# Hybrid decoder layer on one core: the recurrence's half of the output projection moved between the steps of the prompt attention

## The chip, the cores and the metric

One Trainium2 chip, one core. The metric is the device time of one execution in microseconds. A profile of one execution gives the rows below; times in the trace count from its first instruction.

## The reference

One step of a decoder layer for a prompt of 2048 tokens and a sample group of 8 sequences of 8 tokens, in float32, model width 1024:

```
n = rms_norm(x);  proj = n @ w_in
att = dilated_attention(q, k, v)      # 8 heads x 64; windows (128,1), (512,4), (2048,16)
rw  = rwkv7_time_mix(...)             # 8 heads x 64, recurrence over the tokens
h = x + concat(att, rw) @ w_out       # w_out: 1024 x 1024
y = h + relu(rms_norm(h) @ w_mlp1)**2 @ w_mlp2
```

The mixture has 1024 features: 512 from the attention (`att`), 512 from the recurrence (`rw`). The product with `w_out` is a sum over both, so either half can be made alone and added later. Each sample sequence also attends over 2048 cached keys and values.

## The kernel before, in words

Features lie on the 128 partitions, tokens run along the free axis: 2048 prompt tokens and 64 sample tokens, 2112 columns. Products that must keep float32 accuracy are made of two fp32r parts, "high" and "low": hi = round(x), lo = x - hi (`split`: a copy on ScalarE, line 185, a subtraction on VectorE, line 182), and three matmuls hi x hi, hi x lo, lo x hi.

The order of the work is: input projection and recurrence, to about 1200 us; the prompt attention; the output projection with the sample's attention inside it; the feed-forward part. Intermediate results go through DRAM: `mixA` (four panels of 128 features from the attention) and `mixR` (four from the recurrence, complete before the attention begins).

**Prompt attention** (`attention`, line 1053). Four passes p, one for each pair of heads (`ty` 0 and 1), each with three branches b and four groups of token blocks. A step is two blocks of 128 queries in branches 0 and 1, four in branch 2; so a pass has 8 + 8 + 4 = 20 steps, and all passes 80. In a step the scores of a block are made by two matmuls (lines 1084 and 1085, tile `sc`), bias and row minimum on VectorE (line 1087), the exponential on ScalarE (line 185, tile `e`), transposes on TensorE (line 1102, tile `pt`), a copy to SBUF by ScalarE and VectorE in turn (`evac`, tile `pts`), and the product with the values (line 1109, tile `o`). After each step `pump()` draws two pieces of `merge` of the pass before, a generator of about 20 pieces: it weights the three branches by their softmax denominators (matmul line 1197 into the one PSUM buffer of pool `pax`, tile `ax`; products on VectorE, sums on GpSimd, line 1200) and stores to `mixA`. The last pass's merge runs after the loop, on the score banks, and its sums on VectorE. Value tiles `vt` (line 1039) are loaded three ahead into four buffers; the next pass's keys and queries during branches 1 and 2.

**Output projection** (from line 1426 on). Six chunks of 352 columns (`NC_`). `wo_panel` loads and splits a panel of 128 rows of the weight (two of the eight in pool `we` during the last pass, six in the buffers that the last pass's keys leave); `mix_panel` loads and splits a panel of the mixture for one chunk. Each chunk loads the input `xh` into its part of the residual (line 1441), and for each of 8 groups of 128 output features makes 8 panels x 3 = 24 matmuls (line 1451, tile `pwo`, four PSUM buffers), in the order of panels 4 to 7 (recurrence), 0 to 3 (attention); VectorE adds the result to the residual (tile `res`). After each group two pieces of the **sample's attention** are drawn (`sample_all`, line 1312, 8 sequences of 8 pieces). A sequence reads 5 key tiles and 5 value tiles of 512 KB from the cache (`kv`, lines 1255 and 1288; two buffers in pool `sat` and two in `wo2`, in turn) and 8 rows of new values. The last chunk holds the 64 sample columns, so all of the sample comes before it. From the third chunk on the residual is stored to `hD` (line 1457).

All transfers are issued by SP, in one order. The framework's scheduler fixes each engine's order when the program is built, by priority (program order) and a simulated timeline; an engine then works in that order.

Of the kernel before, what the change touches and what calls it, by code (L numbers as in the profile page):

```python
# [171 lines left out]
def _build(ctx, tc, nc, I, O, dbg, upto):  # L172
# [49 lines left out]
    mixR = dram.tile([4, P, T + NS], F32, name="mixR")  # L222
    hD = dram.tile([P, KT, T + NS], F32, name="hD")
# [758 lines left out]
    ar = ph2.enter_context(pool(name="ar", bufs=1))  # L982

# [40 lines left out]
    def bias_load(p, b):  # L1024
        bts = []
        for ty in range(2):
            bt = ae.tile([P, 256], F32, name=f"bt{b}{ty}")
            nc.sync.dma_start(out=bt, in_=bass.AP(tensor=bvD.tensor, offset=bvD.offset + (2 * p + ty) * P * 1152 + b * 384 + 127, ap=[[1151, P], [1, 256]]))
            bts.append(bt)
        return bts  # L1030
# [22 lines left out]
    def attention(p, pump, ahead):  # L1053
# [5 lines left out]
        for b in range(3):  # L1059
# [8 lines left out]
            for grp in range(4):  # L1068
                vp, vt = vt, next_v()
                o = ppo.tile([P, 512], F32, name="o")  # L1070
                for t2 in range(0, 4, 2 if b < 2 else 4):
# [3 lines left out]
                    for ty in range(2):  # L1075
# [4 lines left out]
                        for x, i in enumerate(tl):  # L1080
# [6 lines left out]
                            V.tensor_tensor_reduce(out=e[:, c0:c0 + n], in0=ps[:, c0:c0 + n], in1=bts[ty][:, 256 - n:256], scale=-1.0, scalar=3e38, op0=ALU.add, op1=ALU.min, accum_out=nm)  # L1087
# [36 lines left out]
    def merge(p, ob, st):  # L1124
# [47 lines left out]
        dn = at.tile([P, P], F32, name="dn")  # L1172
        dm = at.tile([P, P], F32, name="dm")
# [52 lines left out]


    kvs = []

    def kv_tile():  # L1230

        kv_tile.n += 1
        pl, bufs = kvs[kv_tile.n % len(kvs)]
        return pl.tile([P, 1024], F32, name="kv", bufs=bufs)
# [86 lines left out]
    woh = [None] * KT  # L1321
    wol = [None] * KT
# [9 lines left out]
    def mix_panel(pl, k, c0):  # L1332

        mh = pl.tile([P, NC_], F32R, name="mh", bufs=5)
        ml = pl.tile([P, NC_], F32R, name="ml", bufs=5)
        src = (mixA if k < 4 else mixR)[k % 4]
        n = min(NC_, (T if k < 4 else NT) - c0)
        mr = we.tile([P, 512], F32, name="mr", tag="raw", bufs=3)
        nc.sync.dma_start(out=mr[:, :n], in_=src[:, c0:c0 + n])
        split(mr[:, :n], mh[:, :n], ml[:, :n])  # L1340
        if n < NC_:
            split(attS[:, k], mh[:, n:], ml[:, n:])
        return mh, ml

    rest = iter(())
    for p in range(4):
        before = rest
        def pump():
            for _ in range(2):
                next(before, None)  # L1350

        rest = attention(p, pump, ahead)
        for _ in before:
            pass
        if p == 2:
            kqa.close()
            we = ph3.enter_context(pool(name="we", bufs=1, side="right"))
            sat = ph3.enter_context(pool(name="sat", bufs=1, side="right"))

# [23 lines left out]
    kvs.append((sat, 2))  # L1383
    for k in (4, 5):
        wo_panel(we.tile([P, 2 * D], F32R, name=f"wo{k}"), k)
    mixed = {}
    for k in range(4, 8):
        mixed[k, 0] = mix_panel(we, k, 0)
# [37 lines left out]
    with pool(name="wo2", bufs=1) as wo2, pool(name="pwo", bufs=4, space=PSUM, side="right") as pwo, pool(name="psa", bufs=1, space=PSUM) as psa, pool(name="pst", bufs=1, space=PSUM) as pst:  # L1426
        kvs.append((wo2, 2))
        sample = sample_all(psa)
        for k in (6, 7, 0, 1, 2, 3):
            wo_panel(kqb.tile([P, T], F32R, name="wo", tag="kq"), k)  # L1430
        order = (4, 5, 6, 7, 0, 1, 2, 3)
        for c0 in range(0, NT, NC_):
# [8 lines left out]
            nc.sync.dma_start(out=h, in_=I["xh"][:, :, c0:c0 + NC_])  # L1441
            for k in order:
                if (k, c0) not in mixed:
                    mixed[k, c0] = mix_panel(we if k >= 4 else wo2, k, c0)
            for o in range(KT):
                ps = pwo.tile([P, 512], F32, name="pwo")
                i = 0
                for k in order:
                    mh, ml = mixed[k, c0]
                    for a, b in ((woh, mh), (woh, ml), (wol, mh)):  # L1450
                        PE.matmul(ps[:, :NC_], a[k][:, o * P:(o + 1) * P], b, start=(i == 0), stop=(i == 3 * KT - 1))  # L1451
                        i += 1
                tt(h[:, o], ps[:, :NC_], h[:, o], ALU.add)
                for _ in range(2):
# [219 lines left out]
```

## Time and profile before

| what | us |
|---|---|
| median of 3 runs | 3351.66 |
| lowest and highest | 3347.38 and 3363.11 |
| the profiled execution | 3357.47 |
| its span, first to last instruction | 3355.7 |

The span leaves out 1.8 us of the profiled execution's own time. A row of a view of groups has line, engine, operation, output and inputs, shapes, the count, then busy time and mean of one, then idle time of the engine before them and what ended it. PE is TensorE's matmuls, PEld its weight loads, which overlap them; DVE, ACT and POOL are VectorE, ScalarE and GpSimd; SPq is SP's queue.

### The profile page before, as it was taken

To read this page: it belongs to the slowest core of one execution; us is meant where nothing else is said; L and a number is where in the kernel's file an instruction comes from. 1 tells how busy PE (TensorE), PEld (TensorE's weight loads), DVE (VectorE), ACT (ScalarE), POOL (GpSimd) and SP (SyncE) were. 2 spreads that over 40 slices of the span, in tenths; PEclk is the share of its full clock that TensorE was granted. 3 is DMA by queue.
4 is the path that set the end of the run, shared out by engine and by line. 5 is a ranking of instruction groups with operands and counts; after the bars stand their busy time and mean duration, and the time that the engine had idled before them with its cause. 6 is when DMAs were issued, how large, how long until landed. Compare 5 with 4: busy or idle time off the path is not lost.

```text
span 3355.7 us, 63761 instructions
## 1 busy us (share of the span) xinstructions
PE 3135.5 (93%) x24214; PEld 2865.0 (85%) x24214; DVE 2157.2 (64%) x4547; ACT 1469.2 (44%) x3497; POOL 976.1 (29%) x1141
## 2 busy tenths in 40 slices
PE   5999899989988979999799689999999999999999
PEld 5876877877787868888688579999899999899999
DVE  4656677677566435656554577676976767967675
ACT  4545566555555446677222233232433323433332
POOL 1003422453044100111000233343533334533332
PEclk9999999999998989999899789999999999999999
DMA  5465575466456383323766322222232222222222
GB/s 169 137 185 149 131 204 158 109 157 178 124 131 178 106 279 117 126 74 90 243 221 235 123 85 89 64 85 64 98 113 64 88 63 86 88 68 84 64 89 73
DMA packets 349144, 418.55 MB, mean 125 GB/s; under 512 B 117252, under 2 KB 210367, under 8 KB 348837
## 3 DMA queue, kind: packets, MB, share of 16 engines
q1 hardware_dynamic: 348836, 414.48, 41.6%
q8 instruction: 190, 3.11, 0.4%
q14 instruction: 118, 0.96, 0.1%
HBM read 325.62 MB, written 93.46 MB: 125 GB/s over the span
## 4 chain that ended last, share of the span: by engine, by line
PE 72%; DMA 9%; DVE 9%; SPq 3%; issue 2%; POOL 2%; ACT 2%; DVEq 0%; POOLq 0%; ACTq 0%
PE pm L1603 20%; PE pm L1557 17%; PE pj L334 7%; PE pwo L1451 5%; PE pj L802 4%; PE o L1109 3%; PE pt L1102 2%; PE sc L1084 2%; PE sc L1085 2%; DVE ml L182 2%; DMA wr<-in_wq 1%; DMA wr<-in_wr 1%; DVE rl L1517 1%; DVE wl L1477 1%; DMA xg<-in_xg 1%
## 5 line engine op out<-in xcount | busy, mean ns | idle before, releaser
L185 ACT ACTIVATE wh<-wr 128x512 fp32r<-128x512 f32 x744 | 463.4, 625 | 818.5 <-PE pm L1603 473.4
L1603 PE MATMUL pm<-fh,wl 128*128 128x352 f32 x1536 | 495.9, 323 | 8.8 <-DVE wl L1477 8.8
L1603 PE MATMUL pm<-fh,wh 128*128 128x352 f32 x1536 | 493.4, 324 | 0.0
L1603 PE MATMUL pm<-fl,wh 128*128 128x352 f32 x1536 | 492.6, 323 | 0.5 <-DVE fl L182 0.5
L1557 PE MATMUL pm<-ml,wh 128*128 128x352 f32 x1344 | 437.0, 325 | 15.1 <-DVE ml L182 15.1
L1557 PE MATMUL pm<-mh,wh 128*128 128x352 f32 x1344 | 438.6, 327 | 9.4 <-ACT mh L185 9.2
L1557 PE MATMUL pm<-mh,wl 128*128 128x352 f32 x1344 | 436.0, 325 | 5.7 <-DVE wl L1477 4.6
L182 DVE TENSOR_TENSOR res<-pm,res 128x352 f32<-128x352 f32 x384 | 198.6, 522 | 287.5 <-PE pm L1603 284.7
L1477 DVE TENSOR_TENSOR wl<-wr,wh 128x512 fp32r<-128x512 f32 x432 | 361.1, 836 | 6.1 <-ACT wh L185 3.5
L1603 PEld LDWEIGHTS pm<-fh,wl 128*128 128x128 f32 x1536 | 290.2, 189 | 9.8 <-DVE wl L1477 9.8
L1603 PEld LDWEIGHTS pm<-fl,wh 128*128 128x128 f32 x1536 | 289.4, 189 | 1.3 <-DVE fl L182 1.1
L1603 PEld LDWEIGHTS pm<-fh,wh 128*128 128x128 f32 x1536 | 289.2, 189 | 0.8 <-ACT fh L185 0.2
L1557 PEld LDWEIGHTS pm<-ml,wh 128*128 128x128 f32 x1344 | 256.5, 191 | 19.1 <-DVE ml L182 19.0
L1557 PEld LDWEIGHTS pm<-mh,wh 128*128 128x128 f32 x1344 | 256.2, 191 | 11.5 <-ACT mh L185 11.5
L1557 PEld LDWEIGHTS pm<-mh,wl 128*128 128x128 f32 x1344 | 255.8, 190 | 8.9 <-DVE wl L1477 7.3
L802 PE MATMUL pj<-wh,nh 128*128 128x256 f32 (+1 forms) x816 | 242.4, 298 | 13.5 <-ACT qn L185 6.7
L802 PE MATMUL pj<-wh,nl 128*128 128x256 f32 (+1 forms) x816 | 241.1, 296 | 2.2 <-DVE nl L182 2.2
L334 PE MATMUL pj<-nh,wh 128*128 128x512 f32 (+3 forms) x600 | 222.8, 374 | 20.4 <-ACT nh L185 10.4
L1481 POOL TENSOR_TENSOR wr<-wr 128x512 f32<-128x512 f32 x48 | 68.9, 1435 | 591.0 <-DVE wl L1477 502.6
L802 PE MATMUL pj<-wl,nh 128*128 128x256 f32 (+1 forms) x816 | 240.7, 296 | 0.0
L182 DVE TENSOR_TENSOR wl<-wr,wh 128x512 fp32r<-128x512 f32 (+1 forms) x216 | 150.2, 698 | 135.2 <-ACT wh L185 130.0
L334 PE MATMUL pj<-nl,wh 128*128 128x512 f32 (+3 forms) x600 | 222.0, 371 | 5.9 <-DVE nl L182 5.9
(312 smaller groups left out, 7262.2 us busy)
## 6 DMA issues: line engine op xcount, KB each, us to landing
wr<-in_w SPq DMA_DIRECT2D x384, 256.0 KB
wr<-in_wr SPq DMA_DIRECT2D x120, 256.0 KB
wr<-in_wq SPq DMA_DIRECT2D x96, 256.0 KB
kv<-in_kc SPq DMA_DIRECT2D x40, 512.0 KB
kv<-in_vc SPq DMA_DIRECT2D x40, 512.0 KB
xsD<-xst SPq DMA_DIRECT2D x56, 256.0 KB
xrkv<-xsD SPq DMA_DIRECT2D x32, 384.0 KB
vt<-vD SPq DMA_DIRECT2D x48, 256.0 KB
```

The lines of the kernel that those rows point to most:

```text
L182: V.tensor_tensor(out, a, b, op)
L185: S.activation(out, in_, func, bias=bias, scale=scale, **kw)
L334: PE.matmul(ps[:m, :n], a[:, k, :m], b[h * 4 + k][:, c0:c0 + n], start=(h == 0 and i == 0), stop=(h == 1 and i == 11))
L802: PE.matmul(out, a[h * 2 + k][:, i * P:i * P + m], b[:, k, :], start=(h == 0 and q == 0 and i % 2 == 0), stop=(h == 3 and q == 5 and (i % ...
L1084: PE.matmul(ps[:, c0:c0 + n], cols(qst, b, i, False), cols(kst, b, i, both), start=True, stop=False)
L1085: PE.matmul(ps[:, c0:c0 + n], cols(qst, b, i, False), cols(klo, b, i, both), start=False, stop=True)
L1109: PE.matmul(o[ty * 64:ty * 64 + 64, (i % 4) * P:(i % 4 + 1) * P], kv[:, ty * 64:ty * 64 + 64], ptss[ty][:, y * P:(y + 1) * P], start=fst, ...
L1451: PE.matmul(ps[:, :NC_], a[k][:, o * P:(o + 1) * P], b, start=(i == 0), stop=(i == 3 * KT - 1))
L1477: (G if pooled else V).tensor_tensor(wl, w, wh.bitcast(F32), ALU.subtract)
L1481: G.tensor_tensor(S[0], A21, A22, ALU.add)
L1557: PE.matmul(ps, a[:, k], b[:, k], start=(n == 0), stop=(n == 11))
L1603: PE.matmul(ps, a[:, f], b[:, cs], start=(i == 0), stop=(i == 11))
```

## The change

A generator `recurrent_half` is added. Twice (for output features 0 to 511 and 512 to 1023) it loads and splits the weight rows of the four recurrence panels, then goes over 8 chunks of 264 columns: it loads and splits the four recurrence panels of the mixture (copy and subtraction both on GpSimd), and for each of 4 groups of output features loads the input, makes 4 x 3 = 12 matmuls into the attention's buffer `ax`, adds the input on VectorE and stores the sum to a new DRAM tensor `rD`. It yields twice for the weights of each half, once after each chunk's loads and once after each product: 2 x (2 + 8 x 5) = 84 times. `pump()` draws it once a step and twice in each eighth; what is left is drawn after the four passes.

The output projection then loads `rD` in place of the input and makes 12 matmuls for each group, over the attention's panels only. Its four weight panels all go into buffers that the last pass's keys leave, after the last merge in program order; two more of these buffers become four more tiles for the sample's cache, so that `kv` has eight. The sample's pieces are drawn 8 for each 5 groups, over five chunks. To make room, the third branch's bias tile is 128 columns wide and two small tiles share buffers of others.

```diff
@@ -220,6 +220,7 @@
     xsD = dram.tile([15, P, T + NS], F32, name="xsD")
     mixA = dram.tile([4, P, T + NS], F32, name="mixA")
     mixR = dram.tile([4, P, T + NS], F32, name="mixR")
+    rD = dram.tile([P, KT, T + NS], F32, name="rD")
     hD = dram.tile([P, KT, T + NS], F32, name="hD")
@@ -980,6 +981,7 @@
     at = ph2.enter_context(pool(name="at", bufs=1))
     ae = ph2.enter_context(pool(name="ae", bufs=1))
     ar = ph2.enter_context(pool(name="ar", bufs=1))
+    fo = ph2.enter_context(pool(name="fo", bufs=1))
     kqb = ph3.enter_context(pool(name="kqb", bufs=6, side="right"))
     kqs = [kqa.enter_context(pool(name="kqa", bufs=6)), kqb]
@@ -1024,8 +1026,9 @@
     def bias_load(p, b):
         bts = []
         for ty in range(2):
-            bt = ae.tile([P, 256], F32, name=f"bt{b}{ty}")
-            nc.sync.dma_start(out=bt, in_=bass.AP(tensor=bvD.tensor, offset=bvD.offset + (2 * p + ty) * P * 1152 + b * 384 + 127, ap=[[1151, P], [1, 256]]))
+            w = 256 if b < 2 else 128
+            bt = ae.tile([P, w], F32, name=f"bt{b}{ty}")
+            nc.sync.dma_start(out=bt, in_=bass.AP(tensor=bvD.tensor, offset=bvD.offset + (2 * p + ty) * P * 1152 + b * 384 + 383 - w, ap=[[1151, P], [1, w]]))
             bts.append(bt)
         return bts
@@ -1169,8 +1172,8 @@
             tt(alike(sc[:, b], b), alike(nall, b), nat(0, b), ALU.subtract)
         act(sc, sc, AF.Exp)
         yield
-        dn = at.tile([P, P], F32, name="dn")
-        dm = at.tile([P, P], F32, name="dm")
+        dn = at.tile([P, P], F32, name="dn", tag="nall2")
+        dm = at.tile([P, P], F32, name="dm", tag="nall")
         tt(dn, sc[:, 0], nat(1, 0), ALU.mult)
         for b in (1, 2):
             tt(alike(dm, b), alike(sc[:, b], b), nat(1, b), ALU.mult)
@@ -1224,14 +1227,52 @@
     G.memset(zst, 0.0)
     mv2 = at.tile([P, 2, 2, 4, 4, 8], F32, name="mv2")
+    FT = 264
+
+    def recurrent_half():
+
+
+        def halves(src, hi, lo):
+            n = src.shape[-1]
+            r = fo.tile([P, FT], F32, name="fr", bufs=3)
+            nc.sync.dma_start(out=r[:, :n], in_=src)
+            G.tensor_copy(hi, r[:, :n])
+            G.tensor_tensor(lo, r[:, :n], hi.bitcast(F32), ALU.subtract)
+
+        for o0 in range(0, KT, 4):
+            w = []
+            for k in range(4):
+                w.append([fo.tile([P, 512], F32R, name=f"fw{x}{k}") for x in "hl"])
+                for c in range(0, 512, 256):
+                    halves(I["wo"][:, 4 + k, o0 * P + c:o0 * P + c + 256], w[k][0][:, c:c + 256], w[k][1][:, c:c + 256])
+                if k % 2:
+                    yield
+            for c0 in range(0, T + NS, FT):
+                m = []
+                for k in range(4):
+                    m.append([fo.tile([P, FT], F32R, name=f"fm{x}", bufs=4) for x in "hl"])
+                    halves(mixR[k, :, c0:c0 + FT], *m[k])
+                yield
+                for o in range(4):
+                    x = fo.tile([P, FT], F32, name="fr", bufs=3)
+                    nc.sync.dma_start(out=x, in_=I["xh"][:, o0 + o, c0:c0 + FT])
+                    ps = pax.tile([P, 512], F32, name="ax")
+                    i = 0
+                    for k in range(4):
+                        for a, b in ((0, 0), (0, 1), (1, 0)):
+                            PE.matmul(ps[:, :FT], w[k][a][:, o * P:(o + 1) * P], m[k][b], start=(i == 0), stop=(i == 11))
+                            i += 1
+                    tt(x, ps[:, :FT], x, ALU.add)
+                    nc.sync.dma_start(out=rD[:, o0 + o, c0:c0 + FT], in_=x)
+                    yield
+
     kvs = []
     def kv_tile():
         kv_tile.n += 1
-        pl, bufs = kvs[kv_tile.n % len(kvs)]
-        return pl.tile([P, 1024], F32, name="kv", bufs=bufs)
+        return kvs[kv_tile.n % len(kvs)]()
     kv_tile.n = -1
@@ -1329,25 +1370,30 @@
             nc.sync.dma_start(out=wr, in_=I["wo"][:, k, o:o + 512])
             split(wr, woh[k][:, o:o + 512], wol[k][:, o:o + 512])
-    def mix_panel(pl, k, c0):
-
-        mh = pl.tile([P, NC_], F32R, name="mh", bufs=5)
-        ml = pl.tile([P, NC_], F32R, name="ml", bufs=5)
-        src = (mixA if k < 4 else mixR)[k % 4]
-        n = min(NC_, (T if k < 4 else NT) - c0)
+    def mix_panel(pl, k, c0, bufs):
+
+        mh = pl.tile([P, NC_], F32R, name="mh", bufs=bufs)
+        ml = pl.tile([P, NC_], F32R, name="ml", bufs=bufs)
+        n = min(NC_, T - c0)
         mr = we.tile([P, 512], F32, name="mr", tag="raw", bufs=3)
-        nc.sync.dma_start(out=mr[:, :n], in_=src[:, c0:c0 + n])
+        nc.sync.dma_start(out=mr[:, :n], in_=mixA[k, :, c0:c0 + n])
         split(mr[:, :n], mh[:, :n], ml[:, :n])
         if n < NC_:
             split(attS[:, k], mh[:, n:], ml[:, n:])
         return mh, ml
     rest = iter(())
+    half = recurrent_half()
+    steps = 0
     for p in range(4):
         before = rest
         def pump():
+            nonlocal steps
             for _ in range(2):
                 next(before, None)
+            steps += 1
+            for _ in range(1 if steps % 8 else 2):
+                next(half, None)
         rest = attention(p, pump, ahead)
         for _ in before:
@@ -1356,6 +1402,8 @@
             kqa.close()
             we = ph3.enter_context(pool(name="we", bufs=1, side="right"))
             sat = ph3.enter_context(pool(name="sat", bufs=1, side="right"))
+    for _ in half:
+        pass
     sbias = sat.tile([P, 136 + 520 + 1288], F32, name="sbias")
     sb1, sb4, sb16 = sbias[:, 0:136], sbias[:, 136:656], sbias[:, 656:]
@@ -1380,12 +1428,10 @@
             G.tensor_copy(qbd[rr, :, p, ty * 8:ty * 8 + 8], qSs[rr, p].rearrange("p (b i) -> p b i", i=8))
     attS = sat.tile([P, 4, NS], F32, name="attS")
-    kvs.append((sat, 2))
-    for k in (4, 5):
-        wo_panel(we.tile([P, 2 * D], F32R, name=f"wo{k}"), k)
+    kvs += [lambda: sat.tile([P, 1024], F32, name="kv", bufs=2)] * 2
     mixed = {}
-    for k in range(4, 8):
-        mixed[k, 0] = mix_panel(we, k, 0)
+    for k in range(3):
+        mixed[k, 0] = mix_panel(we, k, 0, 3)
     for _ in rest:
         pass
     ph2.close()
@@ -1424,11 +1470,14 @@
             G.tensor_tensor(rst[i // 8], q, mhalf[:, 0:8], ALU.pow)
     with pool(name="wo2", bufs=1) as wo2, pool(name="pwo", bufs=4, space=PSUM, side="right") as pwo, pool(name="psa", bufs=1, space=PSUM) as psa, pool(name="pst", bufs=1, space=PSUM) as pst:
-        kvs.append((wo2, 2))
+        for k in range(4):
+            wo_panel(kqb.tile([P, T], F32R, name="wo", tag="kq"), k)
+        for _ in range(2):
+            kvt = kqb.tile([P, T], F32, name="kv2", tag="kq")
+            kvs += [lambda t=kvt[:, i:i + 1024]: t for i in (0, 1024)]
+        kvs += [lambda: wo2.tile([P, 1024], F32, name="kv", bufs=2)] * 2
         sample = sample_all(psa)
-        for k in (6, 7, 0, 1, 2, 3):
-            wo_panel(kqb.tile([P, T], F32R, name="wo", tag="kq"), k)
-        order = (4, 5, 6, 7, 0, 1, 2, 3)
+        owed = 0
         for c0 in range(0, NT, NC_):
             if c0 + NC_ == NT:
                 for _ in sample:
@@ -1438,20 +1487,22 @@
                 res = residual(min(g, 1))
                 res0 = res0 if g else res
             h = res[:, :, q0:q0 + NC_]
-            nc.sync.dma_start(out=h, in_=I["xh"][:, :, c0:c0 + NC_])
-            for k in order:
+            nc.sync.dma_start(out=h, in_=rD[:, :, c0:c0 + NC_])
+            for k in range(4):
                 if (k, c0) not in mixed:
-                    mixed[k, c0] = mix_panel(we if k >= 4 else wo2, k, c0)
+                    mixed[k, c0] = mix_panel(wo2, k, c0, 5)
             for o in range(KT):
                 ps = pwo.tile([P, 512], F32, name="pwo")
                 i = 0
-                for k in order:
+                for k in range(4):
                     mh, ml = mixed[k, c0]
                     for a, b in ((woh, mh), (woh, ml), (wol, mh)):
-                        PE.matmul(ps[:, :NC_], a[k][:, o * P:(o + 1) * P], b, start=(i == 0), stop=(i == 3 * KT - 1))
+                        PE.matmul(ps[:, :NC_], a[k][:, o * P:(o + 1) * P], b, start=(i == 0), stop=(i == 11))
                         i += 1
                 tt(h[:, o], ps[:, :NC_], h[:, o], ALU.add)
-                for _ in range(2):
+                owed += 8
+                while owed >= 5:
+                    owed -= 5
                     next(sample, None)
             if g:
                 nc.sync.dma_start(out=hD[:, :, c0:c0 + NC_], in_=h)
```

## Rows read from the trace of the kernel before

**Rows 1.** The page: busy time by engine, and the chain that ended last, by engine.

```profile
PE 3135.5 (93%) x24214; PEld 2865.0 (85%) x24214; DVE 2157.2 (64%) x4547; ACT 1469.2 (44%) x3497; POOL 976.1 (29%) x1141
...
PE 72%; DMA 9%; DVE 9%; SPq 3%; issue 2%; POOL 2%; ACT 2%; DVEq 0%; POOLq 0%; ACTq 0%
```

**Rows 2.** Windows, stages around the change: stretch, each engine's busy us, granted clock, DMA share, GB/s.

```profile
1248.00:1598.00 350.00, 346.10 (x2764) 289.43 (x2765) 207.27 (x878) 245.87 (x850) 46.82 (x66) 0.98 0.34 104
1598.00:1623.00 25.00, 9.81 (x42) 4.49 (x39) 16.70 (x32) 4.98 (x9) 0.00 (x0) 0.64 0.42 142
1623.00:1873.00 250.00, 235.88 (x2216) 208.12 (x2216) 119.06 (x390) 62.10 (x140) 3.29 (x2) 0.95 0.72 244
1873.00:1899.00 26.00, 25.06 (x144) 24.76 (x144) 4.89 (x14) 1.20 (x5) 0.00 (x0) 0.93 0.06 21
1899.00:1960.00 61.00, 36.88 (x142) 31.24 (x143) 56.98 (x89) 25.77 (x53) 33.92 (x21) 0.64 0.27 76
```

**Rows 3.** Waits of PEld in the attention: who waited for whom, us in total, times, longest.

```profile
PEld pt L1102 <- issue: 19.3, 111, 0.3
PEld o L1109 <- issue: 8.4, 40, 0.4
PEld o L1109 <- ACT e L185: 2.9, 12, 0.4
PEld sc L1084 <- DVE st L1087: 2.6, 10, 0.4
...
PEld sc L1084 <- DVE wo L182: 0.2, 1, 0.2
```

**Rows 4.** Fullest windows of the output stage, and DMA issues (count, size of each).

```profile
1640.00:1660.00 20.00, 20.00 (x192) 19.08 (x191) 7.97 (x27) 4.20 (x10) 0.00 (x0) 1.00 0.89 307
...
1840.00:1860.00 20.00, 17.31 (x195) 13.40 (x196) 8.99 (x29) 4.96 (x12) 0.00 (x0) 0.94 0.87 293
...
kv<-in_kc SPq DMA_DIRECT2D x40, 512.0 KB
kv<-in_vc SPq DMA_DIRECT2D x40, 512.0 KB
...
mr<-mixR SPq DMA_DIRECT2D x24, 176.0 KB
```

**Rows 5.** Timeline of DVE in the last token chunk, evictions of output groups.

```profile
1887.10 0.52 DVE L182 TENSOR_TENSOR res<-pwo,res 128x352 f32<-128x352 f32 x1 [3.35 <-PE pwo L1451]
1890.98 0.52 DVE L182 TENSOR_TENSOR res<-pwo,res 128x352 f32<-128x352 f32 x1 [3.36 <-PE pwo L1451]
```

**Rows 6.** Timeline of PE, two matmuls of 256 columns with eleven others between them.

```profile
629.77 0.28 PE L802 MATMUL pj<-wh,nh 128*128 128x256 f32 x1
...
631.19 0.28 PE L802 MATMUL pj<-wh,nh 128*128 128x256 f32 x1
```

**Rows 7.** Evictions of the buffer ax by DVE, and the merge's sums on POOL.

```profile
L182 DVE TENSOR_TENSOR ob<-ax,ob x36: 680/687/693, 1345.1 to 1563.0; 128x512 f32<-128x512 f32 x36
...
L1200 POOL TENSOR_TENSOR ob<-ob,ob 128x512 f32<-128x512 f32 x24 | 31.0, 1291 | 148.1 <-DVE ob L182 116.3 <-issue 28.7 <-ACT e L185 2.9
```

**Rows 8.** Waits of SP's queue in the attention.

```profile
SPq L1039 <- PE o L1109: 123.6, 26, 17.2
```

**Rows 9.** The chain that ended last, tail of the attention, in order of time.

```profile
1602.08 6.00 DMA raw<-in_wo
...
1609.98 0.29 SPq L1190
...
1610.32 2.81 DMA wrow<-wD
...
1623.21 6.90 PE pwo L1451 x25
```

**Rows 10.** Timeline of ACT: the last two sample sequences scaled.

```profile
1849.01 0.35 ACT L185 ACTIVATE os<-ax,srd 128x128 f32<-128x128 f32 x1
...
1872.13 0.37 ACT L185 ACTIVATE os<-ax,srd 128x128 f32<-128x128 f32 x1 [6.92 <-PE ax L1301]
```

More of the change, by code (lines that the diff above doesn't have):

```diff
@@ L1086, in attention @@
                             nm, dn = st[:, 0, b, i // 4, ty, i % 4:i % 4 + 1], st[:, 1, b, i // 4, ty, i % 4:i % 4 + 1]
-                            V.tensor_tensor_reduce(out=e[:, c0:c0 + n], in0=ps[:, c0:c0 + n], in1=bts[ty][:, 256 - n:256], scale=-1.0, scalar=3e38, op0=ALU.add, op1=ALU.min, accum_out=nm)
+                            V.tensor_tensor_reduce(out=e[:, c0:c0 + n], in0=ps[:, c0:c0 + n], in1=bts[ty][:, bts[ty].shape[1] - n:], scale=-1.0, scalar=3e38, op0=ALU.add, op1=ALU.min, accum_out=nm)
                             act(e[:, c0:c0 + n], e[:, c0:c0 + n], AF.Exp, bias=nm, scale=-1.0, accum_out=dn)
@@ L1320, in _build @@
     SQ = 88
-    woh = [None] * KT
-    wol = [None] * KT
+    woh = [None] * 4
+    wol = [None] * 4
     def wo_panel(w, k):
```

## The prediction

> **What bounds the kernel now.** I read the page first: TensorE (PE) is busy 93% of the span and holds 72% of the chain that ended last [rows 1]. That is a mean over stages, so I cut the span where the change acts [rows 2]: the prompt attention (1248 to 1598 us), its tail (to 1623), the output projection with the sample's attention beside it (to 1873, where the last sample is merged), its last token chunk (to 1899), and the way into the feed-forward part. In the attention PE shows 346 of 350 us busy, but matmul ends are modelled; the row of its weight loads (PEld) is the sharper one, 289.4 us, which leaves 60.6 us. The table of waits says what these are [rows 3]: two rows named "issue" hold 27.7 us in 151 pieces of some 0.18 us, always before a transpose or a probability-times-value product, so they are changes from one array form to another, not waits for work. Fifteen rows name an engine, the largest 2.9 us, together 16.4 us. So the attention is PE's already. In the output stage PE is also full, and the DMA engines stand at 0.72 and 244 GB/s; the fullest stretches reach 307 and 293 GB/s at shares of 0.89 and 0.87 [rows 4].
>
> **The change, part by part. The product itself.** An output group of 24 matmuls of 352 columns takes 3.88 us, the step between two evictions with PE alone at work [rows 5], 0.162 us a matmul. The change takes 12 of 24 out of 48 groups: 576 x 0.162 = 93.1 us off the output stage. It adds 64 products of 12 matmuls of 264 columns. Matmuls of 256 columns follow each other at 1.42/12 = 0.118 us [rows 6]; with 8 of the 96 columns between the two prices, 264 cost 0.122, and 768 of them 93.5 us. **PE work is conserved**; the change wins only where it fills idle time, and loses where it opens some.
>
> **Attention, +87 us.** The loop has 80 steps (4.4 us each) and draws the new generator 90 times; it has 84 yields, so it is used up inside the loop. Of the 93.5 us, what can be absorbed lies between nothing and all 60.6 us of idle weight loading: +33 to +94 us. I take 14, most of the 16.4 us that name work and none of "issue". What can be added: each product stands between other forms, up to two more form changes of 19.3/111 = 0.17 us for 64 products, 22 us; and the products use the one PSUM buffer that the merge of the head pair before also turns over. There an eviction takes 0.69 us at 512 columns [rows 7] and 0.52 at 352 [rows 5], so some 0.43 at 264. About half of the steps hold two merge pieces besides; a product and its eviction take 1.9 us of a step of 4.4 to 5.5, so mostly it fits. I take 8 us between 0 and 22. Sum 93.5 - 14 + 8 = +87 (bounds +33 and +116).
>
> Beside it, off the path: POOL gets 80 pairs of copy and subtract. By its add of 512 columns, 1.29 us [rows 7], 264 columns are 0.67 us and a pair at most 1.33: 107 us, where POOL is busy 47 of 350; cover is ample as throughput. VectorE gets 64 evictions of 0.43, 28 us, beside 207 of 350. DMA gets some 28 MB (weights 2.1, mixture twice 8.7, input 8.7, stored half 8.7), 64 GB/s over some 440 us on top of 104 at a share of 0.34: covered on average. SP issues them in order, behind value-tile loads that wait 123.6 us in 26 pieces, up to 17.2 us, for buffers that PE frees [rows 8]; that is a rival below. The narrower third bias, the shared tags of dn and dm and the smaller lists of panels cost nothing: one short transfer each or none.
>
> **Tail, -4 us.** Here the chain goes through loads of output weights, 6.00 us of one, and the merge's small store and load of its row weights come behind them on SP at 1609.98; PE starts the projection at 1623.21 [rows 9]. After the change the weight panels are asked for after the merge in program order. Between 0 and the 7 us that stand before it I take 4.
>
> **Main stretch, 250 us.** It holds 40 groups of 3.88 (155 us), a quarter of the last chunk (144 of its 192 matmuls come later [rows 2], so 48 x 0.162 = 8 us) and 87 us for eight samples with their form changes. With halved groups PE needs 78 + 87 = 165 us. Then the transfers decide: 80 loads of 512 KB for the cache [rows 4] plus chunks and stores, in all 244 x 250 + 142 x 25 = 64.6 MB from 1598 on, less 20 of the mixture loads of 176 KB (3.6 MB; the input reload is replaced by one of the same size): 61 MB. At 300 GB/s, the fullest stretches, 203 us; at today's 244, 250 us. More cache buffers (eight instead of four) speak for the better end, the in-order queue and the sample's own chain for the worse: the last sample, with PE nearly free, still took 1872.13 - 1849.01 = 23.1 us [rows 10], and eight of these are 185. I take 272, halfway: 224 us from 1598, that is until 1822, so 199 us instead of 250: **-51** (bounds -72 and -25).
>
> **Last chunk.** 8 groups of 1.94 = 15.5 us, and 2 for the sample's split, since now all four panels hold sample columns and nothing can be summed ahead: 17.5 instead of 26, **-8.5**. The way into the feed-forward part stays.
>
> **Sum.** +87 - 4 - 51 - 8.5 = +23.5 us. The profiled execution took 3357.47 us (span 3355.7), so 3381; the median of the runs shown is 5.8 us lower, so **3375 us**.
>
> **A rule against the row.** The rows say that most idle time in the attention is form changes, and my sum leaves it idle. The Trainium skill (Trainium Kernel Development and Optimization, Best Practices) says to judge distance to roofline by the busy share of LDWEIGHTS, not of matmuls. By that rule the attention has 17% to give, and the sum would be +33 there and -31 in all. The trace of before agrees that the matmul row hides the gap; that the gap can be filled, no row shows. It is the first rival.
>
> **The rivals.** (1) *The gaps take the product.* If new matmuls fall into the form changes and the waits, all 60.6 us are absorbed: attention +33, in all -31, **3321**. For it: the clock of 0.98 and the many small pieces. Against: a form change stays one, whatever stands behind it. It decides from the point where over 40 us are absorbed. Chance 0.18. (2) *The output stage reaches its best.* Transfers at 300 GB/s and all of the tail's 7 us: 87 us saved, attention +87, **3352**, no difference. For it: eight cache buffers, and transfers that can start in the tail. Chance 0.20. (3) *The transfers stay at 244 GB/s* and the tail as it is: 25 + 8.5 = 33.5 us saved, so +53.5, **3405**. For it: SP's order and the 23.1 us chain. Chance 0.14. (4) *SP's queue holds the new loads.* A mixture load behind a value load waits 4.75 us in the mean (123.6/26); where that passes the step it was asked ahead, PE, in order, stands. If it hits 8 of the 16 chunks, 38 us: **3413**. Chance 0.10. (5) *The product isn't between the steps*, because the scheduler, which orders by simulated readiness, puts it behind the attention: the same 93.5 us at 1598, of which the tail hides 15 (25 less 9.8 busy): **3367**, little else. It goes with the forecast, which has the remaining 0.38.
>
> **How the numbers follow.** About 0.5% or 17 us can be told from no change by a measurement of this kernel: faster is under 3335, slower over 3368. Faster: rival 1 and a sliver of rival 2, 0.20. Same: most of rival 2 and the lower edge of the forecast, 0.25. Slower: the rest, 0.55. The forecast's own range, with the size of its two unknowns (absorption and transfer rate) each moved by half of its bounds' distance, is 3355 to 3398. The range of 8 in 10 goes on to the edge of rival 1 below and past rivals 3 and 4 above: 3324 to 3418.
>
> **What would show it.** Right: the attention loop ends some 87 us later, with PEld's "issue" rows of much the same size; the output stage up to the last chunk some 55 us shorter, at 260 to 285 GB/s; PEld there under 80% busy; 64 products of 12. Wrong: an attention longer by under 50 us (rival 1); PE rows in it that wait for fm or fr tiles, or for mixR's landing (rival 4); more than 290 GB/s (rival 2) or no more than 250 (rival 3) in the output stage; a feed-forward part whose length moves by over 5 us, for which I have no term.

## The result, and the profile after

The changed kernel takes 3435.91 us (median of 4 runs, 3433.39 to 3445.51) against 3354.72 for the kernel before in the same sets of runs: a ratio of 1.0246 (95% interval 1.0214 to 1.0279). The sign was forecast, the size was not: +81 us instead of +23.5, outside the range, which ended at 3418. The profiled execution took 3436.56 us. In the comparisons below one slow run of score_banks_and_tail, 6739.47 us where its nine others took 3367 to 3379, is left out.

The page's row of busy time and the windows of the stages, cut where the last value product, the first output matmul and the last merged sample lie, answer to [rows 1] and [rows 2]. The last window is a stretch inside the attention.

```profile
PE 3162.9 (92%) x24406; PEld 2877.3 (84%) x24406; DVE 2171.5 (63%) x4579; ACT 1463.8 (43%) x3465; POOL 1064.1 (31%) x1301
```

```profile
1248.00:1762.00 514.00, 470.04 (x3535) 400.79 (x3538) 236.03 (x930) 249.27 (x839) 128.16 (x212) 0.89 0.40 122
1762.00:1791.00 29.00, 15.19 (x87) 6.75 (x79) 20.88 (x53) 5.11 (x11) 0.00 (x0) 0.65 0.60 211
1791.00:1960.00 169.00, 149.37 (x1628) 123.07 (x1628) 98.81 (x340) 48.89 (x110) 3.30 (x2) 0.92 0.86 315
1960.00:1978.00 18.00, 16.11 (x99) 15.61 (x97) 5.26 (x15) 1.56 (x6) 0.00 (x0) 1.00 0.09 30
1397.00:1437.00 40.00, 23.38 (x70) 15.82 (x68) 10.94 (x20) 1.09 (x6) 15.67 (x19) 0.56 0.27 81
```

The output stage did a little better than its forecast: the main stretch 169 us instead of 250, the last chunk 18 instead of 26, the tail 29 instead of 25, together -85 us (forecast -63.5); the tail, forecast at 4 us less, got 4 us longer. The attention grew by 164 us instead of 87. So the spans differ by 164 - 85 = +79 us, and the miss is the attention's 77 us, less the 21.5 us that the output stage gave beyond its forecast. Its weight loads went from 289.4 to 400.8 us, +111, but 113 us of the stretch hold none, where it was 60.6. In the last window ScalarE, which makes every exponential, is busy for 1.09 us of 40: the attention stands still.

What it stands for is in the waits of ScalarE and of GpSimd in the attention (who waited for whom, us in total, times, longest):

```profile
ACT ob L185 <- POOL ob L1203: 92.5, 3, 39.7
```

```profile
POOL fmh L1239 <- PE ax L1263: 109.6, 13, 21.0
```

ScalarE's copy of a branch output (`ob<-o`) waits three times, once for each of the last three passes, for GpSimd's sums in the merge of the pass before; the kernel before has no such row. The timeline around the first of these waits shows the traffic on the buffer `ax` (L1200 is the merge, L1263 the product, DVE `ob` and `fr` their evictions):

```profile
1403.83 0.77 PE L1200 MATMUL ax<-wrow,wsel 128*128 128x512 f32 x1 [4.96 <-DMA wrow<-wD]
...
1408.54 0.80 PE L1200 MATMUL ax<-wrow,wsel 128*128 128x512 f32 x1 [0.78 <-DVE ob L182]
...
1410.21 0.56 PE L1263 MATMUL ax<-fmh,fwh 128*128 128x264 f32 x1 [0.88 <-DVE ob L182]
1410.57 0.42 PE L1263 MATMUL ax<-fml,fwh 128*128 128x264 f32 x1
1410.79 0.42 PE L1263 MATMUL ax<-fmh,fwl 128*128 128x264 f32 x1
...
1413.72 0.79 PE L1200 MATMUL ax<-wrow,wsel 128*128 128x512 f32 x1 [0.53 <-DVE fr L182]
```

```profile
1436.80 1.08 ACT L185 ACTIVATE ob<-o 128x512 f32<-128x512 f32 x2 [38.15 <-POOL ob L1203]
```

Four merge pieces, a product of 12 matmuls, then two pieces and a product in turn, each behind the eviction of the one before, and nothing of the new pass between them. The merge isn't slower than before: from the first to the last of its 12 weighting matmuls this one takes 31.6 us, and 34.2 in the kernel before. It starts late: the first of them stands at 1403.8 us, in the kernel before at 1344.2. Sixteen products stand ahead of this merge in program order, and the timeline has the last matmul of the sixteenth at 1376.9 us; the merge's first matmuls on `ax` follow at 1380.5. (In the kernel before some of these run ahead, during the pass itself, from 1250.2 on.) These are the rows of the tile `ax`, after and before (first and last start in us).

```profile
L1144 PE MATMUL ax<-ident,st x48: 272/273/298, 1380.5 to 1649.9; 128*32 128x128 f32 x48
L1200 PE MATMUL ax<-wrow,wsel x36: 416/794/796, 1403.8 to 1720.2; 128*128 128x512 f32 x36
```

```profile
L1141 PE MATMUL ax<-ident,st x48: 272/273/297, 1250.2 to 1471.2; 128*32 128x128 f32 x48
L1197 PE MATMUL ax<-wrow,wsel x36: 415/481/502, 1344.2 to 1562.5; 128*128 128x512 f32 x36
```

### The profile page after: what moved, and what is told of

It reads as the page before. It is cut to its first block, busy times and chain, and to the rows that moved or that the text cites. A ratio compares the mean times of both kernels' runs of the same rounds, so it can differ in the third digit from the quotient of the medians.

```text
span 3434.8 us, 64761 instructions
## 1 busy us (share of the span) xinstructions
PE 3162.9 (92%) x24406; PEld 2877.3 (84%) x24406; DVE 2171.5 (63%) x4579; ACT 1463.8 (43%) x3465; POOL 1064.1 (31%) x1301
```

## The experiments

The theory, T: the products stand in the order of the one buffer ahead of the merge, and late products make the merge late; branches 1 and 2 have one output tile each (line 1061 of the changed kernel: two only for branch 0), so the next pass's second branch can't be stored until the merge has read the old one, and with two output banks full everything stops. The rivals: S, late inputs (tiles, SP's order) are the cause, and another bank won't help; P, the products' own matmul work is the cost, and the waits only hide it.

**Merge on the score banks.**

```diff
-            return psc.tile(...name="sc") if p == 3 else pax.tile(...name="ax")
+            return psc.tile(...name="sc")
```

> Theory T (one PSUM buffer, taken in order by the products and by the merge, makes the merge late; the next pass's second branch then waits for its output tile, 92.5 us in three waits): with the merge on the score banks the three waits of ScalarE's branch copy on GpSimd's merge sums fall below 15 us in all, the attention loop ends 60 to 90 us earlier (at some 1670 to 1700 us instead of 1762), and the time is 3345 to 3375 us. Rival S (the three input tiles and SP's order make the products late, and the merge's own loads stand behind them on SP): the waits stay above 60 us and the time stays at 3405 to 3440. Rival P (the products' own matmul work is the cost, and the waits only hide it): the waits go, but the loop ends no more than 30 us earlier, time above 3400.

3382.68 us, ratio 1.0076 (1.0053 to 1.0099). The three waits are gone, and the loop ends (start of its last value product) at 1698 us, 63 earlier. The time is 8 us above T's bracket; a control below shows that this place for the merge has a cost of its own.

**Products only when the merge is through.**

```diff
-            nonlocal steps
-            for _ in range(2):
-                next(before, None)
-            steps += 1
-            for _ in range(1 if steps % 8 else 2):
-                next(half, None)
+            left = [next(before, 0) for _ in range(2)]
+            if left[1] == 0:
+                for _ in range(2):
+                    next(half, None)
```

> The products are drawn only in steps in which the merge has no piece left, two at a time; bank and tiles are those of the changed kernel. Theory T: merge and product no longer take turns, so the three waits fall below 25 us and the time is 3345 to 3380. Rival S: products are late for lack of input tiles, so the backlog of a pass still stands ahead of the next merge: waits above 50 us, time 3400 to 3440. Rival P: as the changed kernel within 20 us.

3479.9 us, ratio 1.0372 (1.0348 to 1.0396): worse. The waits are 58.7 us, and ScalarE waits 50.1 us more in the merge's own early pieces. T alone forecast a gain and failed here; S is right as to the backlog, though the time is 40 us above its bracket too. The first pass has no merge before it, so 40 draws fall into it, and what isn't done at its end stands ahead of the merge on the buffer: thirty products, the last at 1438 us, and only then the merge's weighting matmuls, from 1456.7 us on.

**All products behind the attention.**

```diff
             steps += 1
-            for _ in range(1 if steps % 8 else 2):
-                next(half, None)
```

> All products are drawn after the four passes. All theories: the loop ends as in the kernel before, at 1595 to 1605 us, if the products alone cause its +163 us. The 64 products then run behind each other on the one buffer: at the 2.3 us a product seen in the changed kernel where nothing else ran, 147 us, so some 3415 us in all; with rival S, at the 4 to 5 us a product that the input tiles allow, 260 to 320 us, over 3520.

3513.26 us in one run. The loop ends at 1604 us, 5 later than in the kernel before. The products run from 1561 to 1915 us, 5.5 us each, though one with its eviction needs 2.3 where its inputs are there (in the changed kernel three start at 1391.11, 1393.42 and 1395.73 us). That is nearer to S's 4 to 5 us than to 2.3; from 1633 us on matmuls of the output projection stand between them, so it isn't the inputs' rate alone. GpSimd's rows in the stretch from 1604 us on name two reasons: the panel tiles hold one chunk, so the next chunk's splits begin when the last product of the chunk is done, and then the mixture has to land.

```profile
POOL fmh L1239 <- DMA fr<-mixR: 100.3, 35, 16.1
POOL fmh L1239 <- PE ax L1263: 98.0, 8, 23.7
```

**Inputs loaded once.** To see how much of the wait comes from late inputs, the mixture is loaded for the first chunk of each half only, then also the weights for the first half only.

```diff
+            m = []
             for c0 in range(0, T + NS, FT):
-                m = []
-                for k in range(4):
+                for k in range(4 if c0 == 0 else 0):
                     m.append([fo.tile([P, FT], F32R, name=f"fm{x}", bufs=4) for x in "hl"])
                     halves(mixR[k, :, c0:c0 + FT], *m[k])
```

> The changed kernel, with the recurrence's mixture panels loaded and split for the first chunk of each half alone and used for all eight chunks (the other chunks' mixture is left out); the products, their one buffer and the draws are the same. If products are late because each chunk's panels can only be loaded when the last product of the chunk before has freed them (theory S), the backlog goes: the three waits of ScalarE on GpSimd's merge sums fall below 20 us and the time is 3360 to 3390 us. If taking turns on the one buffer makes the merge late by itself (theory T without S), the waits stay above 60 us and the time above 3415.

3391.87 us, ratio 1.0111 (1.0052 to 1.0169); the waits are 39.6 us, between what the two theories said. The gap where the weights change was still there: no matmul of a product between 1447 and 1482 us, and the next product's twelve spread over 9 us. So, on top of that edit:

```diff
+        w = []
+        m = []
         for o0 in range(0, KT, 4):
-            w = []
-            for k in range(4):
+            for k in range(4 if o0 == 0 else 0):
                 w.append([fo.tile([P, 512], F32R, name=f"fw{x}{k}") for x in "hl"])
...
-            m = []
             for c0 in range(0, T + NS, FT):
-                for k in range(4 if c0 == 0 else 0):
+                for k in range(4 if c0 == 0 and o0 == 0 else 0):
```

> The changed kernel (products and merge on the one buffer), with the recurrence's weights and mixture loaded and split once, before the first product, and used for all 64 products (the rest is left out). If late inputs make the backlog and taking turns passes it on to the merge: with no load left after the start, only the start's lateness (the first product 40 to 50 us after the first step) is left; the three waits of ScalarE on GpSimd's merge sums, 92.5 us in the changed kernel and 39.6 with the mixture alone loaded once, fall below 25 us, the wait of the third and fourth pass to none, time 3365 to 3385. If taking turns alone is enough: waits above 35 us, time above 3388.

3376.43 us, ratio 1.0064 (1.0044 to 1.0084), waits 13.9 us, the longest 9.7 in the second pass. The row that was 92.5 us, in these two kernels:

```profile
ACT ob L185 <- POOL ob L1203: 39.6, 3, 29.0
```

```profile
ACT ob L185 <- POOL ob L1203: 13.9, 3, 9.7
```

With each load taken away the wait shrinks, on the same buffer and with the same 64 products. Turn-taking harms little by itself; it is how a product's lateness gets to the merge.

**The transfers without the products** (loads, splits and stores stay; the matmuls and the addition are left out, so the output lacks the recurrence's half).

```diff
-                    ps = pax.tile([P, 512], F32, name="ax")
...
-                    tt(x, ps[:, :FT], x, ALU.add)
                     nc.sync.dma_start(out=rD[:, o0 + o, c0:c0 + FT], in_=x)
```

> The changed kernel without the 64 products and their eviction (the recurrence's half is left out of the sum): loads, splits and stores stay. If the loop's +163 us come from the products and what waits on their buffer, the loop ends at 1595 to 1610 us and the time is 3265 to 3290 us (3354 less some 84 of the output stage). If the transfers and SP's order cost by themselves, the loop ends after 1625 us and the time is over 3300.

3288.31 us, ratio 0.9802 (0.9745 to 0.9859). The loop ends at 1604 us: SP's longer queue, the added transfers and GpSimd's 80 pairs cost the attention some 5 us as long as no product holds their tiles.

**Four cache buffers.**

```diff
-        for _ in range(2):
-            kvt = kqb.tile([P, T], F32, name="kv2", tag="kq")
-            kvs += [lambda t=kvt[:, i:i + 1024]: t for i in (0, 1024)]
```

> The changed kernel with the four added cache buffers taken away (two in each pool as before). If the room brings the output stage's gain beyond the halved product: its transfers fall from 315 to under 270 GB/s and the stage from the first output matmul to the last eviction grows from 186 us to over 205 us; time 3455 or more. If the halved product alone brings it: within 8 us of the changed kernel.

3467.01 us in one run, 31 more than the changed kernel. The windows of its attention and of its main output stretch:

```profile
1248.00:1757.00 509.00, 466.73 (x3532) 398.35 (x3532) 235.60 (x929) 249.29 (x840) 128.57 (x212) 0.90 0.40 123
1783.00:1990.00 207.00, 166.32 (x1687) 128.32 (x1687) 103.90 (x356) 52.11 (x117) 3.30 (x2) 0.82 0.79 275
```

207 us at 275 GB/s instead of 169 at 315: of the 81 us that this stretch gains, 38 hang on the room for the cache.

**Merge on the score banks, controls and combinations.** The kernel before with the same edit, and the first edit with the mixture loaded once:

> The kernel before with its merge on the score banks in all passes, as a control: if the move of the merge is no gain or loss of its own, the time is within 8 us of the kernel before (3347 to 3363 us), and the gain that it gives in the changed kernel comes from what stands in the shared buffer. If the merge hurts the scores' three banks by itself: over 3365.

> Merge on the score banks, and the recurrence's mixture loaded and split for the first chunk of each half alone (the other chunks' mixture is left out). Theory P (what is left of the loop's growth is the products' own matmul work, which finds little idle time): 93 us of matmuls less 10 to 20 of waits, so the loop ends between 1671 and 1683 us and the time is 3350 to 3365 us. If late panels still cost the loop with the merge on the score banks: the gain on that kernel (3383 us) is over 15 us. If neither: 3375 to 3390.

The control gave 3389.86 us, ratio 1.0097 (1.0079 to 1.0115), where I expected no change: the merge on the score banks is a loss of its own, 35 us. Its largest row of TensorE's waits in the attention:

```profile
PE sc L1197 <- DMA wrow<-wD: 15.7, 3, 7.8
```

In order, on a score bank, the merge's matmuls stand in front of the scores while its row weights come through DRAM. The granted clock is lower too, 0.93 over the loop against 0.98 [rows 2]. How the loss divides isn't settled. The windows of the two loops with the merge on the score banks, without the products and with them:

```profile
1248.00:1632.00 384.00, 362.54 (x2795) 300.68 (x2795) 207.96 (x875) 249.34 (x853) 46.51 (x66) 0.93 0.31 96
```

```profile
1248.00:1698.00 450.00, 440.61 (x3502) 381.05 (x3503) 230.80 (x925) 250.94 (x840) 129.20 (x212) 0.99 0.45 138
```

Here the products add 66 us: idle weight loading falls from 83 to 69 us, and the clock is higher with them than without. The combination gave 3377.67 (1.0071, 1.0053 to 1.0089), 5 us below the plain edit and within the intervals of both: with the merge away from the buffer, late panels matter little. Its loop ends at 1698 us too, not at 1671 to 1683 as P had it for this base, which left the merge's own loss out. Two more attempts on this base, products left over for the tail, and two chunks' panels at a time:

```diff
-            for _ in range(1 if steps % 8 else 2):
+            for _ in range(1 if steps % 10 else 0):
```

> Merge on the score banks, and the generator drawn in nine steps of ten, so that 12 draws (some 10 products) are left for the tail, where TensorE is idle for 19 of 30 us. If the tail can take them: the loop ends 12 to 18 us earlier than with the merge on the score banks alone (1680 to 1686 instead of 1698 us), the tail grows by under 6 us, and the time is 3365 to 3375 us. If the tail's transfers, not TensorE, set its length and the products come in front of the merge: no gain, 3378 to 3395.

```diff
-    FT = 264
+    FT = 192
...
-                    m.append([fo.tile([P, FT], F32R, name=f"fm{x}", bufs=4) for x in "hl"])
+                    m.append([fo.tile([P, FT], F32R, name=f"fm{x}", bufs=8) for x in "hl"])
...
-            for _ in range(1 if steps % 8 else 2):
+            for _ in range(2 if steps % 5 in (0, 2) else 1):
```

(and `fr` with four buffers, `e` and `pts` with three, weights in pieces of 128 columns)

> Merge on the score banks; the recurrence's half in 11 chunks of 192 columns with two chunks' panels at a time (eight pairs of tiles instead of four) and four staging tiles, paid for with three instead of four buffers for the exponentials and for the transposed tiles; the generator is drawn seven times in five steps. All of the computation is done. If the panels' supply is what remains above the matmul work: 3350 to 3370 us. If the matmul work is all of it, 1056 matmuls of 192 columns cost some 98 us instead of 93: 3380 to 3395. If the buffers taken away are needed: over 3395.

The first gave 3370.99 us (median of nine runs), ratio 1.0054 (1.0034 to 1.0074), a time as forecast for a tail that takes the products; but the loop's end stayed at 1698 us, and the intervals overlap with the plain edit's, so no gain is shown. The second gave 3397.48 (1.0122, 1.0105 to 1.0140): more matmuls and fewer buffers together cost more than earlier panels give, and the run can't tell which of the two it is.

**A buffer of their own for the products**, taken from the scores, with its control, and taken from the outputs.

```diff
-    psc = ph2.enter_context(pool(name="psc", bufs=3, ...))
+    psc = ph2.enter_context(pool(name="psc", bufs=2, ...))
+    pfo = ph2.enter_context(pool(name="pfo", bufs=1, space=PSUM))
...
-                    ps = pax.tile([P, 512], F32, name="ax")
+                    ps = pfo.tile([P, 512], F32, name="fx")
```

> The changed kernel with a PSUM buffer of their own for the products, taken from the scores (two banks instead of three); the merge keeps its buffer to itself. Theory T (turns on one buffer make the merge late): the three waits of ScalarE on GpSimd's merge sums fall below 15 us, and without the 35 us that the merge on the score banks cost the kernel before, the time is 3345 to 3375 us, less what two score banks cost (its control says). If late products hold TensorE's own order up, wherever they land: waits or idle of TensorE before products over 40 us, time above 3390.

> The kernel before with two instead of three banks for the scores, as a control for the run beside it. If the third bank is only spare: within 8 us of the kernel before (3347 to 3363 us). If the scores of the next step need it: the attention's 350 us grow by 10 to 40, 3365 to 3395 us.

3379.41 us (1.0064, 1.0042 to 1.0087) and 3375.35 (1.0049, 1.0033 to 1.0064). No wait of ScalarE on the merge's sums is left. The windows of both attentions:

```profile
1248.00:1703.00 455.00, 451.31 (x3552) 386.24 (x3549) 235.68 (x939) 254.58 (x853) 127.47 (x212) 1.00 0.46 142
```

```profile
1248.00:1616.00 368.00, 360.75 (x2799) 296.80 (x2795) 211.19 (x882) 250.72 (x857) 46.41 (x66) 0.97 0.32 100
```

Same banks for the attention, so the difference is the products with their transfers: 455 - 368 = 87 us of time, 89 us of weight loads; idle weight loading is 71 us without them and 69 with them. The granted clock is 0.97 without and 1.00 with them, so at an equal clock they could cost more, at most 0.03 x 368 = 11 us by my estimate from these rows.

The same with the bank from the outputs (`ppo` with one buffer, `psc` again with three):

```diff
-    ppo = ph2.enter_context(pool(name="ppo", bufs=2, space=PSUM, side="right"))
+    ppo = ph2.enter_context(pool(name="ppo", bufs=1, space=PSUM, side="right"))
```

> The products on a PSUM buffer of their own, taken from the attention's outputs (one bank instead of two); scores keep three. The loop's growth is then the matmul work (about 88 us, as two score banks against their control show: 1703 against 1616 us) plus what one output bank costs: a copy of 0.59 us and two crossings between engines in each of 48 groups, some 40 us at most, 10 where other work of TensorE fills it. 3355 to 3375 us if filled; 3375 to 3400 if not; a copy that waits for the merge then also holds the values' products, so a late merge would cost more than before.

3367.7 us, ratio 1.0026 (1.0009 to 1.0043): the best version with the move, and by its interval 3 to 14 us slower than the kernel before. Its loop ends at 1693 us, 95 after the kernel before, and the main output stretch takes 171 us, as in the changed kernel (169).

```profile
1248.00:1693.00 445.00, 441.93 (x3542) 384.57 (x3543) 235.35 (x944) 257.18 (x865) 124.07 (x206) 0.99 0.48 145
1724.00:1895.00 171.00, 150.77 (x1628) 124.34 (x1628) 99.59 (x341) 49.03 (x110) 3.31 (x2) 0.91 0.86 311
```

## Why the prediction was wrong, step by step

**Right: PE's work is conserved.** The attention was PE's already. With a buffer of their own the 64 products cost 87 us against the control, where the step put 93.5 - 14 + 8 = 87. That the figures agree is in part luck: of the 14 us of absorption that runs shows 2, the 8 us for the shared buffer had no place in it, and the clock differs. The rival that the gaps take the product (in all -31 us) is out: the loop grew by 87 us and not by 33. The "issue" row before the transposes [rows 3] is after the change

```profile
PEld pt L1105 <- issue: 18.4, 105, 0.4
```

so the form changes stayed, as forecast. Waits for work can be filled: with the merge on the score banks 14 us of idle weight loading went. The Trainium skill (Trainium Kernel Development and Optimization, Best Practices) says to judge the distance to roofline by LDWEIGHTS' busy share, which it names beside MFU (the share of TensorE's peak rate that the kernel reaches), and not by that of matmuls. The trace agrees that the matmul row hides idle time (346 of 350 us busy against 289.4); that the part of it in form changes can be filled, no run here shows.

**Right in sum, mis-sized in its parts: the output stage.** -85 us, where -63.5 was taken and -87 was the bound. The tail was wrong in sign, +4 us for -4. The main stretch gained 81 us, past the bound of 72: from the loop's end on the transfers moved (211 x 29 + 315 x 169) / 198 = 300 GB/s, what I took as the best end and priced as rival 2, and by the sign stated for it ("more than 290 GB/s") this is rival 2's output stage. four_cache_buffers shows that the deeper buffers, which I named but priced with a halfway rate, carry 40 of the 71 GB/s by which the stretch is faster (244 before, 275 without them, 315). Rival 2's whole sum, +87 - 87 or no difference, is also what the best version comes near to, 9 us above its kernel before.

**Wrong: the term for the shared buffer, 8 us between 0 and 22.** The step said: "a product and its eviction take 1.9 us of a step of 4.4 to 5.5, so mostly it fits". That counts how full the buffer is, and counts it short. The loop begins at 1222.3 us and not at 1248, so a step is 376/80 = 4.7 us; products in a row start 2.3 us apart and merge pieces 1.3 (in mixture_loaded_once at 1549.60, 1550.93 and 1552.21 us), so a step with a product and two pieces needs the buffer for 2.3 + 2 x 1.3 = 4.9 us. It doesn't mostly fit: it is full. But fullness isn't what cost most, since weights_and_mixture_once has the same turns and waits 13.9 us. The buffer is also an order: whoever stands late in it holds all behind. The runs put +164 - 87 = 77 us there, and the two runs with the inputs loaded once show the mechanism: 92.5, 39.6 and 13.9 us of waiting, and 3436, 3392 and 3376 us. I asked what the bank costs, and not who is queued behind it (the merge), nor who waits for the merge (the next pass's second branch, through one output tile). The premise under it was that loads and splits are "covered on average" and "ample as throughput": with one set of panel tiles they are a chain of their own. The same premise priced rival 5, the products behind the attention, at 3367 us; products_behind_attention took 3513.

The trace before had the sign. This is ScalarE of the kernel before, once in each of the last three passes:

```profile
1379.66 1.06 ACT L185 ACTIVATE ob<-o 128x512 f32<-128x512 f32 x2
...
1470.33 1.06 ACT L185 ACTIVATE ob<-o 128x512 f32<-128x512 f32 x2
...
1563.69 1.05 ACT L185 ACTIVATE ob<-o 128x512 f32<-128x512 f32 x2
```

and GpSimd's last row before the first of them:

```profile
1377.95 1.29 POOL L1200 TENSOR_TENSOR ob<-ob,ob 128x512 f32<-128x512 f32 x1 [0.15 <-DVE ob L182]
```

Two branch outputs are copied in one go (x2), 0.4 us after a merge sum has ended at 1379.24. So two finished output groups already held both output banks until the merge was through, while TensorE found other work (PE 9.77 of the 10 us from 1370 on). There was little slack in that chain, and a delay of 60 us in the merge had to come out in large part: 38 us of waiting in that pass.

**Near: the rival of SP's queue.** It asked for late inputs and priced them at 38 us. The inputs were late, but the queue by itself isn't why: transfers_without_products has the same transfers in it and loses 5 us. Panel tiles and weights hold one set each, so that a split waits for the last product. SP's order then adds to it, since a store that waits for its product holds the loads behind it. In the attention of the changed kernel:

```profile
SPq L1266 <- DVE fr L182: 96.8, 40, 9.2
```

```profile
POOL fmh L1239 <- DMA fr<-mixR: 72.6, 34, 14.7
```

How much of the lateness is the tiles and how much SP's order, no run separates. The cost came by the merge, not by TensorE standing before a product for its inputs: TensorE's rows of waits before a product name the buffer's evictions (9.0 us the largest), and those that name a panel are 0.4 us or less.

## What to carry to other kernels

A PSUM buffer that two streams take in turn is a queue: ask of each stream not only how long it holds the buffer but how late it can come, and who waits behind it. Before work is put into such a queue, look in the trace for what is fed by it with no slack; two outputs of one kind copied right behind a release are a sign of that. And where an engine is full in both stages, moving its work between them can only win what opens elsewhere, here transfers, and that gain needs buffers as well as time.

## What the runs showed of the hardware that was not expected

The stall also slowed the work in it, since TensorE's clock fell. In the stretch 1397 to 1437 us the granted clock is 0.56: full up to 1400 us, at the lower of its two levels (1.2 and 2.4 GHz) from 1402 us on. It fell within 5 us without a matmul (1398.9 to 1403.8) and stayed down while pieces of a few matmuls stood between waits. The product's matmuls in it follow each other at 1410.79 - 1410.57 = 0.22 us instead of 0.12, and the merge's weighting matmuls take 794 ns in the median instead of 481. Over the attention the granted clock is 0.89 against 0.98 [rows 2], and 1.00 in own_buffer_two_score_banks, where ScalarE never waits for the merge's sums.

The other surprise is the DMA rate: 315 GB/s over 169 us, more than the 307 of [rows 4]. But those 20 us aren't the fullest of the kernel before: windows cut elsewhere show more, so 300 GB/s was no limit that its trace had set.

```profile
1630.00:1670.00 40.00, 40.00 (x354) 36.13 (x356) 16.74 (x51) 7.95 (x18) 0.00 (x0) 1.00 0.94 325
```
